# Copying two query tiles out of PSUM ahead of their 1/rms, and a 1/rms formed with tokens on the partitions

## The chip, the cores and the metric

The kernel runs on one core of a Trainium2 chip. The metric is the device time of one execution in microseconds, as the median of several executions. One further execution was taken by the hardware profiler; its rows are the ones quoted below, and their times count from the start of its span.

## What is computed

One step of one decoder layer for two sets of tokens that share the weights: a prompt of 1024 tokens and 64 sample tokens (8 sequences of 8), with 1024 channels in fp32. Cut to what matters here:

```
h = RMSNorm(x)
q, k, v, gmlp_u, gmlp_v, gate_attn, gate_gmlp = split(h @ w_in)
A = sliding-window attention (window 128, grouped queries, a learned sink per head)
B = gelu(gmlp_u) * (W_s LayerNorm(gelu(gmlp_v)) + b)      in chunks of 128 positions
x = x + (sigmoid(gate_attn) * (A @ w_pa) + sigmoid(gate_gmlp) * (B @ w_pb)) @ w_out
x = x + ConvFFN(RMSNorm(x))         up-projection, causal convolution of width 3, gelu gate, down
y = RMSNorm(x)
```

RMSNorm divides each token's row by the root of the mean of its squares: 1/rms is one number per token.

## The kernel before

Activations lie transposed: channels on the 128 partitions, in 8 tiles, and tokens along the free dimension. The 1088 tokens are two groups: group 0 has the 64 sample tokens and 512 of the prompt (576), group 1 the other 512. Each product is made three times, from operands split in a high and a low part (`wh`, `wl` for weights, `hm` for normed inputs), so a tile of 128 output channels takes 24 matmuls (`mm3`, L198 to L206). Weights come through class `Weights` (L71): SP loads a raw tile (`wraw`), ScalarE casts it to `wh` (L39), VectorE subtracts for `wl` (L40). Three raw buffers and four pairs of split buffers go round.

The norm of the inputs is split in two. The gain is put on the inputs at once (`h_of`, L344), and 1/rms, which is the same for all output channels, is put on the products when they leave PSUM. `norm1` (L350) makes it: a matmul with a matrix of ones sums the squares over the channels into every partition (`sc`, L320), ScalarE takes the root (L321), VectorE the reciprocal (L322); for the tiles that have tokens on the partitions, one-column matmuls (`pt`, L355) give the same with four columns (L356, L357).

For each group the order is: 8 query tiles, 2 key tiles (`K0`), values as token-major tiles (L500, tokens on the partitions, `vst`), then attention with the 16 gate tiles as filling between its steps, the gMLP branch, the merge, and the output projection, which leaves x1 (`x1_tile`, L891) and the running sum of its squares in `nacc`. The accumulators of these products come from a pool of two (`acc2`, L245, tiles `mm`). Sums and copies that leave PSUM land in a pool of four staging tiles (`stage`, L242, `stg`).

In group 0, tiles 0 and 1 are copied out of PSUM by ScalarE (L434), `norm1` is called, and then L446 multiplies the copies by 1/rms and 1/8. In group 1 there is no copy. Both tiles run seven eighths of their products, then the last eighth of each (which needs the last of the normed inputs), `norm1` is called, and L446 reads both tiles from PSUM. After query tile 4 of group 1, `rstd_of` (L456) also forms the second norm's 1/rms of group 0, in `nacc0`.

That is needed by the half sums (`half_sums`, L550): four pieces, each with two tiles `hx` loaded from x1 of group 0 (L557), multiplied by gain and 1/rms (L558), combined by GpSimd and VectorE into `ht` (L220 to L223) and stored. They stand among the gate tiles in the text.

The up-projection follows as block products in seven instead of eight (the sums of weight blocks, `ws`, are made by GpSimd, L150; seven products of 12 matmuls in `Chain.product`, L1041, with up to three of eight PSUM banks `st` per chain). The first three pairs of channels (`FEW`) run for group 0 alone, because the inputs of group 1 are still being made: after the third product, `rstd_last` (L967) forms the second 1/rms of group 1 with two 512-column matmuls by ones, a root and a reciprocal of 128x512, and `t1_pieces` (L974) hands out twelve pieces, one behind each later product, which multiply the eight tiles `x1g` by gain and 1/rms (L982), make sums and split them.

The text gives the order only roughly. The framework's scheduler puts each engine's instructions into one fixed order ahead of the run, and each engine works its own queue in that order. An instruction that waits holds up all that is behind it on its engine, on SP's queue too, from which all the large DMAs are issued. The program's order after the build can be read for both kernels.

## Time and profile before

| | |
|---|---|
| median of 3 runs | 1667.56 us (1667.0 to 1672.0) |
| profiled execution, its own time | 1669.62 us |
| its span, first to last instruction | 1667.6 us |
| mean granted TensorE clock | 0.988 |
| instructions | 27566 |
| HBM traffic over the span | 165.40 MB read, 39.00 MB written |

The profile names engines PE (TensorE matmuls), PEld (its weight loads), DVE (VectorE), ACT (ScalarE), POOL (GpSimd) and SP (the queue that issues DMAs). A row of the timeline gives start and length in us, engine, line, operation, output and inputs, shapes and count; in square brackets stands how long the engine had been idle and what ended that. The view of waits gives who waited for whom: total, times, longest. A row of one line's view gives the shortest, median and longest duration in ns. An fp32 matmul runs as two passes, and so shows twice the count of instructions in the rows of L320, L355, L969 and L970.

### The profile page before, as it was taken

How to read it: one execution, taken by the hardware profiler on the slowest of the kernel's cores; microseconds unless marked ns; L12 is line 12 of the kernel's file. 1: busy time of each engine (PE TensorE's matmuls, PEld its weight loads, DVE VectorE, ACT ScalarE, POOL GpSimd, SP SyncE). 2: the span in 40 equal slices, each digit the busy share in tenths (PEclk: the TensorE clock that was granted, in tenths of full speed). 3: DMA queues.
4: the chain of work that ended last, by engine and by line, in shares of the span. 5: the costliest groups of instructions: out<-in, count | busy, mean ns of one | idle time of the engine just before them, and what ended most of it. 6: DMA issues, size and time to landing. Idle time of an engine off the chain costs nothing.

```text
span 1667.6 us, 27566 instructions
## 1 busy us (share of the span) xinstructions
PE 1614.9 (97%) x10912; PEld 1505.8 (90%) x10912; DVE 1043.2 (63%) x1430; ACT 769.0 (46%) x1492; POOL 442.8 (27%) x520
## 2 busy tenths in 40 slices
PE   8999999999989999999998999999999999999997
PEld 8989999999977888898877989999989999999886
DVE  8546863654467677565466777777777778345433
ACT  6435653333343466444344455545555556344231
POOL 1302230100321344210025555555455541000101
PEclk9999999999989999999999899999999999999998
DMA  5332223144646332424472322231232217744421
GB/s 192 117 115 80 86 86 130 50 150 130 205 137 205 104 101 89 140 83 130 154 255 87 113 104 83 89 106 70 77 105 79 78 62 261 253 149 136 156 91 57
DMA packets 80977, 204.22 MB, mean 122 GB/s; under 512 B 9296, under 2 KB 15504, under 8 KB 80848
## 3 DMA queue, kind: packets, MB, share of 16 engines
q1 hardware_dynamic: 80704, 202.45, 36.3%
q8 instruction: 86, 1.41, 0.3%
q14 instruction: 43, 0.35, 0.1%
q10 hardware_dynamic: 144, 0.01, 0.0%
HBM read 165.40 MB, written 39.00 MB: 123 GB/s over the span
## 4 chain that ended last, share of the span: by engine, by line
PE 77%; DVE 9%; POOL 4%; ACT 4%; DMA 3%; issue 2%; SPq 0%; DVEq 0%; POOLq 0%; ACTq 0%
PE mm L205 30%; PE st L1051 21%; PE dn L1164 15%; PE mm L505 6%; DVE wl L40 2%; POOL ws L150 2%; ACT s L696 1%; PE sc L681 1%; PE po L729 1%; DMA wraw<-wt 1%; POOL pl L717 1%; ACT wh L39 1%; PE mm L817 1%; PE pt L706 1%; DMA traw<-t0d 1%
## 5 line engine op out<-in xcount | busy, mean ns | idle before, releaser
L205 PE MATMUL mm<-hm,wh 128*128 128x320 f32 (+2 forms) x1920 | 430.5, 333 | 13.6 <-DVE stg L446 6.3
L1051 PE MATMUL st<-th,wh 128*128 128x288 f32 (+1 forms) x1232 | 360.7, 293 | 13.7 <-ACT k L1036 12.5
L40 DVE TENSOR_TENSOR wl<-wraw,wh 128x512 fp32r<-128x512 f32 (+3 forms) x279 | 264.7, 965 | 163.5 <-ACT wh L39 159.8
L1051 PE MATMUL st<-th,wl 128*128 128x288 f32 (+1 forms) x1232 | 358.7, 291 | 5.8 <-DVE wl L40 5.8
L39 ACT CAST wh<-wraw 128x512 fp32r<-128x512 f32 (+3 forms) x279 | 210.9, 772 | 330.1 <-PE mm L205 126.5
L1051 PE MATMUL st<-tl,wh 128*128 128x288 f32 (+1 forms) x1232 | 359.1, 292 | 0.0
L205 PEld LDWEIGHTS mm<-hm,wh 128*128 128x128 f32 x1920 | 303.1, 190 | 42.8 <-DVE stg L446 6.7
L205 PE MATMUL mm<-hm,wl 128*128 128x320 f32 (+1 forms) x960 | 265.2, 330 | 0.0
L1164 PE MATMUL dn<-gr,wh 128*128 128x288 f32 (+3 forms) x1088 | 253.1, 324 | 2.3 <-ACT z L1072 2.3
L1051 PEld LDWEIGHTS st<-th,wh 128*128 128x128 f32 x1232 | 236.8, 192 | 16.9 <-ACT k L1036 14.4
L1051 PEld LDWEIGHTS st<-th,wl 128*128 128x128 f32 x1232 | 236.6, 192 | 6.5 <-DVE wl L40 6.5
L1051 PEld LDWEIGHTS st<-tl,wh 128*128 128x128 f32 x1232 | 236.6, 192 | 0.3 <-issue 0.2
L1164 PEld LDWEIGHTS dn<-gr,wh 128*128 128x128 f32 x1088 | 183.1, 188 | 16.3 <-ACT z L1072 2.5
L1164 PE MATMUL dn<-gr,wl 128*128 128x288 f32 (+3 forms) x544 | 175.8, 323 | 0.0
L205 PEld LDWEIGHTS mm<-hm,wl 128*128 128x128 f32 x960 | 159.8, 190 | 14.9
L1164 PEld LDWEIGHTS dn<-gr,wl 128*128 128x128 f32 x544 | 102.3, 188 | 7.0
L505 PE MATMUL mm<-w2h,hm 128*128 128x256 f32 x576 | 104.4, 283 | 1.1 <-DVE vst L44 0.8
L40 DVE TENSOR_TENSOR wl<-ws,wh 128x512 fp32r<-128x512 f32 x100 | 87.2, 888 | 15.4 <-ACT wh L39 14.1
L150 POOL TENSOR_TENSOR ws<-wraw 128x512 f32<-128x512 f32 x50 | 83.3, 1667 | 33.5 <-DVE wl L40 18.2
L505 PEld LDWEIGHTS mm<-w2h,hm 128*128 128x128 f32 x576 | 89.7, 191 | 2.0 <-DVE vst L44 1.0
L1080 DVE SCALAR_TENSOR_TENSOR c<-z,cw,c 128x1104 f32<-128x1104 f32 x44 | 72.7, 1653 | 21.1 <-ACT c L1079 21.1
L205 PE MATMUL mm<-qo,wh 128*128 128x320 f32 (+2 forms) x384 | 84.6, 328 | 0.2 <-DVE stg L825 0.2
(220 smaller groups left out, 2366.4 us busy)
## 6 DMA issues: line engine op xcount, KB each, us to landing
wraw<-wt SPq DMA_DIRECT2D x160, 512.0 KB
wraw<-wt SPq DMA_DIRECT2D x90, 256.0 KB
gd<-z SPq DMA_DIRECT2D x22, 544.0 KB
graw<-gd SPq DMA_DIRECT2D x22, 288.0 KB
wraw<-wpb SPq DMA_DIRECT2D x16, 384.0 KB
graw<-gd SPq DMA_DIRECT2D x22, 256.0 KB
gate<-stg SPq DMA_DIRECT2D x16, 288.0 KB
stg<-gate SPq DMA_DIRECT2D x16, 288.0 KB
```

What stands on the lines that cost most here:

```text
L39: S.copy(hi, src)
L40: V.tensor_sub(lo, src, hi.bitcast(F32))
L150: G.tensor_add(t, x, y)
L205: PE.matmul(ps[:, lo:lo + c1 - c0], u[:, k, :], v[:, c0:c1], start=(k == 0 and i == 0), stop=(k == nk - 1 and i == 2))
L505: PE.matmul(ps, u[:, lo:lo + P], v[:, k, :], start=(k == 0 and i == 0), stop=(k == KD - 1 and i == 2))
L681: PE.matmul(ps[:, h, o0:256], q, kst[kv][:, e, k0:cur + P], start=e == 0, stop=e == 1)
L696: S.activation(s[:, h], s[:, h], AF.Exp, bias=nm[:, h:h + 1], accum_out=dn[:, h:h + 1])
L706: PE.transpose(pt[:, h * P:h * P + P], s[:, h, 0:P], ident)
L717: G.affine_select(t.rearrange("p (h q) -> p h q", h=4), src.bitcast(F32).rearrange("p (h q) -> p h q", h=4), [[0, 4], [-sign, P]], ALU.is_ ...
L1051: PE.matmul(ps, u[:, kk, :], v, start=first and kk + i == 0, stop=kk == 3 and i == 2, skip_group_check=True)
L1080: V.scalar_tensor_tensor(c, z[:, 1:1105], cw[:, i, 1:2], c, ALU.mult, ALU.add)
L1164: PE.matmul(ps, u[:, c, :], v[:, lo:hi], start=f + i == 0, stop=f == NFF - 1 and i == 2, skip_group_check=True)
```

## The change

Two edits. In group 1, query tile 0 now runs all its products, `norm1` is called, and tile 1 runs; ScalarE copies each of the two tiles to a staging tile, in both groups, and VectorE multiplies the copies:

```diff
+                if g == 1:
+                    w2, ps2, f2 = [W.get()], [acc2(), acc2()], []
+                    mm3(ps2[0], chunks, w2[0], hs, 0, KD, KD)
+                    norm1(pro)
+                    w2.append(W.get())
+                    mm3(ps2[1], chunks, w2[1], hs, 0, KD, KD)
+                for c in range(2):
+                    f2.append(stage(n))
+                    S.copy(f2[c], ps2[c][:, base:base + n])
                 if g == 0:
-                    for c in range(2):
-                        f2.append(stage(n))
-                        S.copy(f2[c], ps2[c][:, base:base + n])
-                else:
-                    w2, ps2, f2 = [W.get()], [acc2(), acc2()], []
-                    mm3(ps2[0], chunks, w2[0], hs, 0, KD - 1, KD)
-                    w2.append(W.get())
-                    mm3(ps2[1], chunks, w2[1], hs, 0, KD - 1, KD)
-                    for c in range(2):
-                        mm3(ps2[c], chunks, w2[c], hs, KD - 1, KD, KD)
-                        f2.append(stage(n))
-                norm1(pro)
+                    norm1(pro)
                 for c in range(2):
-                    src = f2[c] if g == 0 else ps2[c][:, base:base + n]
-                    V.scalar_tensor_tensor(f2[c], src, 0.125, rs, ALU.mult, ALU.mult)
+                    V.scalar_tensor_tensor(f2[c], f2[c], 0.125, rs, ALU.mult, ALU.mult)
                     q_tile(c, f2[c])
```

In `rstd_last`, the sums of squares are formed as one column per 128 tokens, with tokens on the partitions, so that root and reciprocal have a shape of 128x4. ScalarE then scales the identity matrix by each column, and a matmul with ones spreads the four diagonals over all partitions, into a PSUM bank that the eight multiplications of `t1_pieces` read:

```diff
         def rstd_last():
-            ps = psu.tile([P, 512], F32, name="st")
-            PE.matmul(ps, ones, nacc, start=True, stop=False)
-            PE.matmul(ps, ones, late["sq"], start=False, stop=True)
-            S.activation(nacc, ps, AF.Sqrt, bias=eps, scale=1.0 / D)
-            V.reciprocal(nacc, nacc)
+            ps, rt = psu.tile([P, 512], F32, name="st"), up.tile([P, 4], F32, name="rt", bufs=1)
+            for i in range(4):
+                for x in (nacc, late["sq"]):
+                    PE.matmul(ps[:, i:i + 1], x[:, i * P:i * P + P], ones[:, 0:1], start=x is nacc,
+                              stop=x is not nacc)
+            S.activation(rt, ps[:, 0:4], AF.Sqrt, bias=eps, scale=1.0 / D)
+            V.reciprocal(rt, rt)
+            rs = psu.tile([P, 512], F32, name="st")
+            for i in range(4):
+                S.activation(nacc[:, i * P:i * P + P], ident, AF.Copy, scale=rt[:, i:i + 1])
+                PE.matmul(rs[:, i * P:i * P + P], ones, nacc[:, i * P:i * P + P], start=True, stop=True)
+            return rs
```

The bank is handed to `t1_pieces` as `rs_last`, and `norm` in it multiplies by `rs_last` where it had `nacc`.

More of the change, by code (lines that the diff above doesn't have):

```diff
@@ L967, in rstd_last, with t1_pieces @@
         def rstd_last():
-            ps = psu.tile([P, 512], F32, name="st")
-            PE.matmul(ps, ones, nacc, start=True, stop=False)
-            PE.matmul(ps, ones, late["sq"], start=False, stop=True)
-            S.activation(nacc, ps, AF.Sqrt, bias=eps, scale=1.0 / D)
-            V.reciprocal(nacc, nacc)
-        def t1_pieces():
+            ps, rt = psu.tile([P, 512], F32, name="st"), up.tile([P, 4], F32, name="rt", bufs=1)
[10 more added lines that the diff above has]
+            return rs
+        def t1_pieces(rs_last):
             t4 = [traw().rearrange("p (k j c) -> p k j c", k=2, j=4) for _ in range(2)]
@@ L981, in norm @@
             def norm(k):
-                V.scalar_tensor_tensor(x1g[k], x1g[k], gains[:, 1, k:k + 1], nacc, ALU.mult, ALU.mult)
+                V.scalar_tensor_tensor(x1g[k], x1g[k], gains[:, 1, k:k + 1], rs_last, ALU.mult, ALU.mult)
                 return x1g[k].rearrange("p (h c) -> p h c", h=2)
@@ L1097, in layer @@
                 if f == 0 and j == 2:
-                    rstd_last()
-                    rest = t1_pieces()
+                    rest = t1_pieces(rstd_last())
                 if rest and 7 * f + j > 3:
```

## The prediction

> **What bounds the kernel now.** The page comes first: which engine fills the span.

> ```profile
> PE 1614.9 (97%) x10912; PEld 1505.8 (90%) x10912; DVE 1043.2 (63%) x1430; ACT 769.0 (46%) x1492; POOL 442.8 (27%) x520
> ```

> TensorE is busy for 97% of the 1667.6 us span, so time can be won only where TensorE stands still or runs slowly. The view of waits, for TensorE, says where that is (total, times, longest):

> ```profile
> PE st L1051 <- ACT k L1036: 12.5, 8, 4.0
> PE mm L205 <- DVE stg L446: 6.3, 1, 6.3
> ...
> PE mm L505 <- DVE vst L44: 0.8, 1, 0.8
> ```

> The 6.3 us of the second row is the longest single wait of all. It lies at the start of the second group. Rows of the timeline there (start, length, engine, line):

> ```profile
> 474.86 0.63 PE L205 MATMUL mm<-hm,wh 128*128 128x512 f32 x2
> 485.37 1.99 ACT L39 CAST wh<-wraw 128x1024 fp32r<-128x1024 f32 x2 [6.08 <-PE mm L205]
> 486.11 1.02 PE L320 MATMUL sc<-pacc,c_ones 128*128 128x512 f32 x2
> 486.97 0.95 PE L355 MATMUL pt<-c_ones,pacc 128*128 128x1 f32 x8
> 489.39 3.35 DVE L322 RECIPROCAL nrs<-nrs 128x512 f32<-128x512 f32 x1 [0.58 <-ACT nrs L321]
> 489.51 1.21 PE L320 MATMUL sc<-nacc,c_ones 128*128 128x320 f32 x4 [1.59 <-ACT rst L356]
> 492.70 3.72 DVE L322 RECIPROCAL nacc<-nacc 128x576 f32<-128x576 f32 x1
> 496.34 1.22 DVE L446 SCALAR_TENSOR_TENSOR stg<-mm,nrs 128x512 f32<-128x512 f32 x2
> 497.02 0.80 PE L205 MATMUL mm<-hm,wh 128*128 128x512 f32 x1 [6.30 <-DVE stg L446]
> ```

> Both accumulators of the pool hold query tiles 0 and 1, and only L446 empties them. L446 needs 1/rms, and on VectorE it stands behind two reciprocals (3.35 and 3.72 us). So tile 2 starts at 497.02, after 1.59 and 6.30 us of idle TensorE. The table of windows (busy time of PE, PEld, DVE, ACT, POOL; granted clock; DMA) adds what follows the idle time:

> ```profile
> 486.10:497.00 10.90, 3.03 (x15) 1.92 (x13) 9.97 (x7) 4.13 (x6) 0.00 (x0) 0.76 0.30 97
> 497.00:502.00 5.00, 4.98 (x12) 3.92 (x13) 4.84 (x7) 2.46 (x4) 1.30 (x1) 0.50 0.11 33
> 560.00:700.00 140.00, 138.63 (x703) 114.24 (x702) 99.03 (x163) 80.57 (x215) 49.61 (x80) 1.00 0.30 102
> 894.90:925.70 30.80, 23.13 (x152) 21.96 (x150) 26.58 (x35) 15.05 (x33) 15.66 (x18) 0.88 0.18 64
> ```

> From 497 to 502 the granted clock is 0.50: half of 5.0 us, 2.5 us, is lost a second time. From 560 on TensorE is full (138.63 of 140 us), so what is won before stays won. The last row is the place of the other edit: there VectorE is busy for 26.58 of 30.80 us and TensorE for only 23.13, so VectorE's queue sets the pace.

> **Part one: the first two query tiles.** Tiles 0 and 1 are 48 products from 474.86 to 486.11: 0.234 us each, 5.63 us a tile. The norm's products end 0.95 us after 486.97, at 487.92: 1.81 us. In the order as built, tile 0 now runs whole, then the norm's products, then tile 1. Tile 0 reaches its last eighth at about 479.8, and the operands for that are ready at 477.85:

> ```profile
> 472.61 5.24 DVE L44 SCALAR_TENSOR_TENSOR hm<-x,c_gains,hm 128x512 fp32r<-128x512 f32 x6
> L434 ACT COPY stg<-mm x2: 641/642/642, 20.2 to 21.0; 128x576 f32<-128x576 f32 x2
> ```

> So tile 0 ends at 480.5, the norm's products at 482.3, tile 1 at about 488.0. ScalarE casts one weight tile (1.0 us, released at tile 0's end), then copies tile 0; the first group's copies took 0.64 us (second row), so the accumulator is free by 482.2. Tile 2 therefore starts at 488.0, right behind tile 1, instead of 497.02: **9.0 us**. Tile 1's copy stands behind one cast and is done by 489.9; tile 3 needs that at 493.6. With the idle time goes the half clock: **2.5 us**. The two products of the first group's norm (1.21 us), until now inside the idle time, go behind tile 4: **+1.2 us**. The two copies cost nothing, because ScalarE is busy for 4.13 of the 10.90 us of the first window; without that cover they would cost 1.3 us.

> The 3.35 us reciprocal is not removed: it starts near 484.1 and ends at 487.4, under tile 1. What each query tile asks of VectorE, from the view that groups instructions (count, busy, mean ns):

> ```profile
> L40 DVE TENSOR_TENSOR wl<-wraw,wh 128x1024 fp32r<-128x1024 f32 x10 | 12.5, 1259 | 6.8 <-ACT wh L39 6.8
> L420 DVE TENSOR_TENSOR qo<-stg,qo 64x512 fp32r<-64x512 f32 x16 | 12.1, 756 | 0.5
> L453 DVE SCALAR_TENSOR_TENSOR stg<-mm,nrs 128x512 f32<-128x512 f32 x6 | 4.1, 686 | 0.9 <-PE mm L205 0.8
> ```

> One subtraction of weights, two of L420 and one evacuation are 3.5 us in 5.63 us of products, so the query tiles themselves are not late. What is late next is the half sums of the first group (hx, ht; L553 to L564). The build moves the reciprocal of nacc behind tile 4 and all eight hx behind tile 6; before, the first ran right behind the idle time. VectorE's order there becomes: tile 6, hx, hx, ht, tile 7, ht, hx, K tile 0, hx, ht, ht, K tile 1, hx, vst, vst, hx, ht, ht, vst, hx, vst. Each hx from the third on waits for a reload of its buffer, with the evacuations queued behind it. The chain of waits and the timeline show such reloads, and what one did:

> ```profile
> 503.91 3.21 DMA hx<-x1d
> 533.06 5.66 DMA hx<-x1d
> 538.81 0.82 DVE L558 SCALAR_TENSOR_TENSOR hx<-hx,c_gains,nacc 128x576 f32<-128x576 f32 x1 [3.08 <-DMA hx<-x1d]
> 540.38 0.70 PE L205 MATMUL mm<-hm,wh 128*128 128x512 f32 x2 [1.20 <-DVE stg L453]
> 548.26 3.47 POOL L465 CAST kst<-kst 64x1024 fp32r<-64x1024 f32 x2 [3.45 <-DVE kst L464]
> 553.56 6.02 PE mm L505 x48
> ```

> A reload takes 3.3 or 5.7 us with its issue, and the long one cost TensorE 1.20 us. I step through the new order with both. TensorE ends tile 6 at 517.3, tile 7 at 523.0, K tile 0 at 528.6, K tile 1 at 534.2, and a token-major tile takes 3.0 us (half of the last row). With 3.3 us, the hx before K tile 0 ends at 529.4, the one before K tile 1 at 533.6. GpSimd's half sum is queued behind two kst copies (3.47 us) and ends at 536.4, so K tile 1 is evacuated at 538.0. Token-major tile 1 needs that accumulator at 537.2: a stall of 0.8. The hx ahead of the first vst makes the next, 0.9. Sum 1.7 us. With 5.7 us the same steps give 2.8 and 2.9, sum 5.7 us. The old stalls of this stretch (1.20 and the 0.8 at vst, 2.0 us) go with the old order.

> Part one: −9.0 −2.5 +1.2 −2.0 = −12.3 us, plus 1.7 or 5.7: −10.6 or −6.6 us. Both reloads have been seen; I take the middle, **−8.6 us**.

> [...]

> **Part two: the second 1/rms.** Rows of the timeline, and two of single lines:

> ```profile
> 893.06 1.02 PE L969 MATMUL st<-nacc,c_ones 128*128 128x512 f32 x2
> 894.37 0.70 PE L1051 MATMUL st<-th,wh 128*128 128x288 f32 x1
> 896.63 0.46 DVE L1062 TENSOR_TENSOR z<-ku,st 128x288 f32<-128x288 f32 x1 [1.73 <-PE st L1051]
> 897.00 3.35 DVE L972 RECIPROCAL nacc<-nacc 128x512 f32<-128x512 f32 x1
> 904.25 1.21 DVE L40 TENSOR_TENSOR wl<-ws,wh 128x512 fp32r<-128x512 f32 x1
> 912.53 0.40 PE L1051 MATMUL st<-th,wh 128*128 128x288 f32 x1 [1.10 <-ACT kn L1038]
> 917.16 0.61 PE L1051 MATMUL st<-th,wl 128*128 128x288 f32 x1 [3.97 <-DVE wl L40]
> L982 DVE SCALAR_TENSOR_TENSOR x1g<-x1g,c_gains,nacc x8: 737/744/1229, 900.4 to 922.0; 128x512 f32<-128x512 f32 x8
> ```

> ```profile
> L357 DVE RECIPROCAL rst<-rst x2: 120/126/131, 28.3 to 492.7; 128x5 f32<-128x5 f32 x1, 128x4 f32<-128x4 f32 x1
> L492 ACT COPY kout<-stg x2: 298/298/298, 547.7 to 550.9; 128x128 f32<-128x128 f32 x2
> ```

> Removed: 3.35 us of reciprocal, for one of 0.12 (L357, the same shape). Added: eight one-column products, 16 passes of 0.12 (8 in 0.95 us at L355), 1.9 us in place of the 1.3 from 893.06 to 894.37; with a change of kind of product the next one moves to about 895.3. The built order then sets a chain. VectorE first takes z, which waits for that product's bank (897.4, was 896.6), then the reciprocal (898.0). ScalarE scales four 128x128 tiles (0.3 each by L492: 899.2). TensorE multiplies them by ones, four products of two passes in among others, about 0.3 to 0.4 each (an estimate from the 0.12 a pass and the gaps around L969): 900.7. So 1/rms is ready **0.3 us later** than before (897.00 + 3.35), although 3.2 us of reciprocal are gone. What is won is that VectorE does the subtraction of 904.25 (1.21 us) while it waits. Its queue, which ends the wait at 917.16, moves by −1.2 +0.4 = **−0.8 us**. Bounds: at best the whole −3.2 us; at worst +1.0, since ScalarE's built order puts kn, for which TensorE waited until 912.53, behind two weight casts, so that the rest of that product starts only near 916.7. I stay near the step by step value.

> The norms (L982) now read 1/rms from PSUM. L453 reads PSUM at 0.69 and L982 takes 0.74: nothing.

> [...]

> **Sum.** −8.6 −0.8 = −9.4 us. The profiled execution took 1669.62 us (span 1667.6), which gives 1660.2; the median of the runs is 1667.56, and I give the forecast against that: **1658.2 us**.

> **Rivals.** (a) *No new stall to speak of*, and part two at its best: −10.6 −3.2, 1653.8 us. For it: SP's new order fetches ten weight tiles ahead of the reloads, so these meet less traffic. Against it: the 5.66 us row. Chance 0.14. (b) *A stall halves the clock*: reloads of 5.7 us, and one stall near 3 us is followed by 5 us at 0.50, as at 497: −6.6 +2.5 −0.8 = −4.9, 1662.7 us. Against it: no stall under 3 us in the rows above is followed by a lower clock. [...] (c) *It doesn't do what it says*: ScalarE's first copy slips behind the table load and square root, or VectorE evacuates tile 2 only after tile 4 is due at 499.2, and TensorE still waits some 6 us: −3, 1664.6 us. The built order speaks against it. Chance 0.06. (d) *Slower*: the half sums, ahead of the K and V evacuations, become the bound. From 3.3 to 5.7 us of reload the stalls grow by 4.0, so 1.7 per us; all that is won (12.3 −1.7 +0.8 = 11.4) is eaten at 3.3 + 6.7 = 10.0 us, and from there the kernel is slower. At 13 us: 1.7 × 3.0 = +5.1, and 2.5 for the clock: 1675.2 us. No row shows over 5.7. Chance 0.04.

> **How the numbers follow.** The forecast has what is left, 0.64; with its own bounds one at a time (reloads of 3.3 to 5.7, part two from −3.2 to +1.0) it spans 1655.8 to 1660.2, and with the long reload and +1.0 together 1662.0. The range takes in (a) and (b): 1653 to 1663 us; (c) and (d), 0.10, stay out. What a measurement of this kernel can tell from no change is about 0.3%, 5.0 us. Faster by more than that: the forecast, (a) and half of (b), 0.84. Within it: the rest of (b) and (c), 0.12. Slower: 0.04.

> **What would show it.** In the profile after: tile 2's first product right behind tile 1's last, with a granted clock of 1.00, or part one is wrong; new waits of L205 and L505 behind hx in the K and V tiles, 1.7 to 5.7 us in all; the norms starting no sooner after the L969 products than before; the wait now ending at 917.16 ending at most 1 us earlier against its neighbours. What would make the forecast wrong: a wait of over 3 us left before tile 2, stalls over 6 us in the V tiles, or part two off by more than 3 us.

## The result, and the profile after

The changed kernel took 1660.53 us (median of 5, 1657.29 to 1662.08) against 1667.56 us before, 7.0 us less by these medians. The ratio over all runs is 0.9951 with an interval of 0.9933 to 0.9969, which is 8.2 us less (5.2 to 11.2). The prediction was 1658.2 us with a range of 1653 to 1663. A second series on another chip (e4_changed_again) gave 0.9943 (0.9930 to 0.9956), 9.5 us less. The profiled execution took 1662.08 us, its span 1660.1.

The page's first row, and rows of the view of waits for TensorE (total, times, longest):

```profile
PE 1616.0 (97%) x10932; PEld 1508.4 (91%) x10932; DVE 1040.6 (63%) x1430; ACT 770.4 (46%) x1498; POOL 438.7 (26%) x520
```

```profile
PE st L1056 <- ACT k L1041: 15.3, 6, 4.1
PE st L1056 <- DVE wl L40: 2.3, 4, 1.0
PE st L1056 <- ACT kn L1043: 1.7, 1, 1.7
PE sc L678 <- DVE s L684: 0.6, 1, 0.6
```

TensorE is as busy as before (1616.0 against 1614.9 us) in a span that is 7.5 us shorter. The row of 6.3 us behind L446 is gone. New is the wait of 0.6 us at a step of attention (L684). The wait behind `kn` is 1.7 us where it was 1.10, the waits for `k` come to 15.3 us where they came to 12.5, and the longest wait for a weight's `wl` is 1.0 us where it was 3.97. Lines have moved: L446 is now L443, L505 L502, L1051 L1056, L982 L987.

**The first place.** Timeline of after (start, length, engine, line; in brackets the idle time before and what ended it):

```profile
476.59 0.63 PE L205 MATMUL mm<-hm,wh 128*128 128x512 f32 x2
483.13 0.58 ACT L439 COPY stg<-mm 128x512 f32<-128x512 f32 x1
485.74 3.35 DVE L322 RECIPROCAL nrs<-nrs 128x512 f32<-128x512 f32 x1 [1.26 <-ACT nrs L321]
```

and the table of windows of after (busy time of PE, PEld, DVE, ACT, POOL; granted clock; DMA):

```profile
482.20:490.00 7.80, 7.80 (x37) 6.17 (x36) 5.30 (x4) 4.08 (x6) 0.00 (x0) 1.00 0.27 102
490.00:502.00 12.00, 12.00 (x52) 9.62 (x52) 8.63 (x12) 6.91 (x11) 0.00 (x0) 1.00 0.25 88
```

The reciprocal of 3.35 us runs under query tile 1, and TensorE has no idle time at all from 482 to 502, at a clock of 1.00. Before, the same stretch held 1.59 + 6.30 us of waiting and 5 us at 0.50.

**The second place.** Timeline of after, from the last evacuation ahead of the norms to the wait that stands at its end in both kernels (969.39 before, after 4.00 us of waiting, at 80.91 us from the start of its L895 at 888.48):

```profile
880.33 0.69 DVE L892 TENSOR_TENSOR x1g<-stg,mm 128x512 f32<-128x512 f32 x1 [3.73 <-PE mm L205]
888.90 0.17 DVE L972 RECIPROCAL rt<-rt 128x4 f32<-128x4 f32 x1
889.11 1.28 ACT L975 ACTIVATE nacc<-c_ident,rt 128x128 f32<-128x128 f32 x4
891.03 1.41 DVE L987 SCALAR_TENSOR_TENSOR x1g<-x1g,c_gains,st 128x512 f32<-128x512 f32 x2 [1.28 <-PE st L976]
914.51 0.40 PE L1056 MATMUL st<-th,wh 128*128 128x288 f32 x1 [2.79 <-ACT k L1041]
958.26 0.61 PE L1056 MATMUL st<-th,wh 128*128 128x288 f32 x1 [4.11 <-ACT k L1041]
```

From L892 to that end are now 77.93 us, 2.98 less. The first norm starts 10.70 us behind L892, where it started 11.90 us behind it (888.48 to 900.38): 1.2 us sooner, not later.

### The profile page after: what moved, and what is told of

Its sections match the earlier page's. It is cut to its first block, busy times and chain, and to the rows that moved or that the text cites. A ratio compares the mean times of both kernels' runs of the same rounds, so it can differ in the third digit from the quotient of the medians.

```text
span 1660.1 us, 27618 instructions
## 1 busy us (share of the span) xinstructions
PE 1616.0 (97%) x10932; PEld 1508.4 (91%) x10932; DVE 1040.6 (63%) x1430; ACT 770.4 (46%) x1498; POOL 438.7 (26%) x520
## 4 chain that ended last, share of the span: by engine, by line
PE 79%; DVE 8%; POOL 5%; ACT 4%; issue 3%; DMA 1%; SPq 0%; DVEq 0%; POOLq 0%; ACTq 0%
PE mm L205 32%; PE st L1056 21%; PE dn L1168 16%; PE mm L502 6%; DVE wl L40 2%; POOL ws L150 2%; ACT s L693 1%; PE sc L678 1%; PE po L726 1%; ACT wh L39 1%; DMA wraw<-wt 1%; POOL pl L714 1%; PE mm L814 1%; POOL ph L714 1%; PE pt L703 1%
## 5 line engine op out<-in xcount | busy, mean ns | idle before, releaser
L205 PE MATMUL mm<-hm,wh 128*128 128x320 f32 (+2 forms) x1920 | 429.8, 332 | 5.7 <-ACT hm L43 5.1
L1056 PE MATMUL st<-th,wh 128*128 128x288 f32 (+1 forms) x1232 | 360.8, 293 | 17.2 <-ACT k L1041 15.3
L39 ACT CAST wh<-wraw 128x512 fp32r<-128x512 f32 (+3 forms) x279 | 210.9, 772 | 348.4 <-PE mm L205 128.3
L40 DVE TENSOR_TENSOR wl<-wraw,wh 128x512 fp32r<-128x512 f32 (+3 forms) x279 | 265.5, 968 | 161.4 <-ACT wh L39 157.8
L1056 PE MATMUL st<-th,wl 128*128 128x288 f32 (+1 forms) x1232 | 359.4, 292 | 2.3 <-DVE wl L40 2.3
L1056 PE MATMUL st<-tl,wh 128*128 128x288 f32 (+1 forms) x1232 | 359.2, 292 | 0.0
L205 PEld LDWEIGHTS mm<-hm,wh 128*128 128x128 f32 x1920 | 302.5, 190 | 34.2 <-ACT hm L43 5.1
L205 PE MATMUL mm<-hm,wl 128*128 128x320 f32 (+1 forms) x960 | 265.0, 330 | 0.0
L1056 PEld LDWEIGHTS st<-th,wh 128*128 128x128 f32 x1232 | 237.2, 193 | 19.9 <-ACT k L1041 16.9
L1056 PEld LDWEIGHTS st<-th,wl 128*128 128x128 f32 x1232 | 236.9, 192 | 3.4 <-DVE wl L40 3.4
L1056 PEld LDWEIGHTS st<-tl,wh 128*128 128x128 f32 x1232 | 237.0, 192 | 0.0
L205 PEld LDWEIGHTS mm<-hm,wl 128*128 128x128 f32 x960 | 159.4, 190 | 14.6
L502 PE MATMUL mm<-w2h,hm 128*128 128x256 f32 x576 | 104.4, 283 | 2.1 <-DVE vst L44 1.2
L40 DVE TENSOR_TENSOR wl<-ws,wh 128x512 fp32r<-128x512 f32 x100 | 87.6, 892 | 16.6 <-ACT wh L39 15.3
L502 PEld LDWEIGHTS mm<-w2h,hm 128*128 128x128 f32 x576 | 89.8, 191 | 2.6 <-DVE vst L44 1.4
L150 POOL TENSOR_TENSOR ws<-wraw 128x512 f32<-128x512 f32 x50 | 81.7, 1634 | 37.6 <-DVE wl L40 21.0
L205 PE MATMUL mm<-qo,wh 128*128 128x320 f32 (+2 forms) x384 | 85.1, 330 | 0.2 <-DVE stg L822 0.2
```

Of the source, the lines that this page charges most:

```text
L39: S.copy(hi, src)
L40: V.tensor_sub(lo, src, hi.bitcast(F32))
L150: G.tensor_add(t, x, y)
L205: PE.matmul(ps[:, lo:lo + c1 - c0], u[:, k, :], v[:, c0:c1], start=(k == 0 and i == 0), stop=(k == nk - 1 and i == 2))
L502: PE.matmul(ps, u[:, lo:lo + P], v[:, k, :], start=(k == 0 and i == 0), stop=(k == KD - 1 and i == 2))
L1056: PE.matmul(ps, u[:, kk, :], v, start=first and kk + i == 0, stop=kk == 3 and i == 2, skip_group_check=True)
```

## The experiments

The executions of one kernel lie 3 to 11 us apart, and such differences arise far from the change too. So two times were read off each profiled execution besides the ratio to the kernel before. *Start* is the start of the last x1 evacuation (L895, in other kernels L892): what the first edit has won by then. *Stretch* is the time from there to the end of the wait of 4 us (969.39 before): what the second edit wins at its place.

| run | what | median us | ratio (interval) | start | stretch |
|---|---|---|---|---|---|
| before | | 1667.56 | | 888.48 | 80.91 |
| after | both edits | 1660.53 | 0.9951 (0.9933 to 0.9969) | 880.33 | 77.93 |
| e4_changed_again | both edits | 1661.35 | 0.9943 (0.9930 to 0.9956) | 878.96 | 77.87 |
| e8_before_again | none | 1671.88 | 0.9999 (0.9989 to 1.0009) | 889.08 | 81.29 |
| e1_tiles_alone | edit 1 | 1665.34 | 0.9959 (0.9947 to 0.9971) | 880.38 | 81.32 |
| e6_copies_alone | only the copies | 1661.41 | 0.9940 (0.9925 to 0.9955) | 880.29 | 81.47 |
| e3_order_alone | only the order | 1660.90 | 0.9937 (0.9925 to 0.9949) | 876.91 | 81.37 |
| e2_rms_alone | edit 2 | 1667.30 | 0.9976 (0.9965 to 0.9986) | 887.94 | 78.38 |
| e5_order_and_rms | order, edit 2 | 1657.92 | 0.9914 (0.9898 to 0.9929) | 877.86 | 78.71 |
| e10_order_rms_hx_two | the same again | 1656.54 | 0.9909 (0.9893 to 0.9925) | 877.53 | 78.52 |
| e9_changed_hx_two | both, `hx` twice | 1659.07 | 0.9926 (0.9913 to 0.9939) | 882.36 | 78.10 |
| e7_reciprocal_twice | one reciprocal more | 1673.97 | 1.0012 (1.0002 to 1.0022) | 890.73 | 85.68 |
| e11_rms_norms_from_sbuf | edit 2, norms from SBUF | 1670.99 | 0.9996 (0.9984 to 1.0008) | 893.45 | 78.83 |
| e12_norms_sbuf_again | the same again | 1669.47 | 1.0001 (0.9989 to 1.0013) | 888.33 | 78.70 |

The kernel before had medians of 1670.05 to 1672.14 on these chips, and each ratio is to runs on its own chip. Four groups stand out. The start has a median of 888.8 in the six kernels with the old first place, 880.3 in the five with copies (8.5 us sooner) and 877.5 in the three with the order alone (11.3 sooner). The stretch is on average 81.3 (80.9 to 81.5) with the old 1/rms and 78.3 (77.9 to 78.7) with the new one read from PSUM: 3.0 us.

A part of every start is chance, because it is there before the changed place is reached: the first product of group 1's tile 0, at 474.86 before, came between 474.45 and 479.20 in the 14 traces. Counted from that product, the last x1 evacuation follows after 413.5 us with the old first place (412.4 to 414.3), after 404.0 with the copies (403.6 to 404.1) and after 400.6 with the order alone (400.5 to 402.2). So edit 1 wins 9.5 us at its place, and the order alone 12.9.

### The two edits apart, and the pair again

e1_tiles_alone has the diff's first hunk and leaves `rstd_last` and `t1_pieces` as before:

> The first edit alone (the two query tiles), the second 1/rms as before. Theory A (the prediction's part one): tile 2 starts right behind tile 1, the last x1_tile addition ends some 9 us earlier than in the kernel before, and since nothing behind it is changed all of that stays: 1658 to 1659 us, ratio 0.9945 to 0.995. Rival B: the up-projection behind it gives back a part of whatever arrives early, so this kernel is no faster than the changed one: 1660.5 us or more. Rival C: both edits share the gain, and this one alone brings 4 to 6 us: 1662 to 1664 us.

e2_rms_alone has the other hunks and leaves the query tiles as before:

> The second edit alone (1/rms with tokens on the partitions), the query tiles as before. In the changed kernel's trace the place itself came out 3 us earlier than the rest (last long VectorE wait of TensorE at 914.5 against 925.7, 11.1 us, of which 8.1 were there before it), and about 3 to 4 us were lost again between 1070 and 1190 us. Theory A: the win stays in part: 1665 to 1667 us, ratio 0.9985 to 0.9995. Rival B: what it wins is given back whole in the up-projection: 1667.6 us, ratio 1.000. Rival C: the loss behind it is larger than the win: over 1669 us.

e4_changed_again is the changed kernel once more:

> The changed kernel once more, for a second trace and a second ratio on the same chip as the other three. If the loss of 3 to 4 us between 1070 and 1190 us is a property of the change, it shows again at the same place, and the ratio is 0.995 again; if it is chance of one execution, the lead of some 11 us at 960 us stays or varies, and the ratio may come out at 0.994 to 0.997.

Measured: edit 1 wins 6.9 us (4.8 to 8.9, from the ratio times 1671.67), edit 2 wins 4.0 us (2.3 to 5.9), both together 9.5 us (7.4 to 11.7). Within the intervals the parts add up. Edit 1 is about what the prediction gave it (8.6), though its ratio, 0.9959, falls short of the 0.9945 to 0.995 expected. Edit 2 is by its ratio, 0.9976, worth more than the 0.9985 to 0.9995 expected, and several times the predicted 0.8 us. The loss between 1070 and 1190 us showed again in e4_changed_again, at the same place; the sum further below comes back to it.

### What the copies are for

e3_order_alone keeps edit 1's order of products but reads both tiles from PSUM, as before. Its diff is against the kernel before:

```diff
                         S.copy(f2[c], ps2[c][:, base:base + n])
+                    norm1(pro)
                 else:
                     w2, ps2, f2 = [W.get()], [acc2(), acc2()], []
-                    mm3(ps2[0], chunks, w2[0], hs, 0, KD - 1, KD)
+                    mm3(ps2[0], chunks, w2[0], hs, 0, KD, KD)
+                    norm1(pro)
                     w2.append(W.get())
-                    mm3(ps2[1], chunks, w2[1], hs, 0, KD - 1, KD)
+                    mm3(ps2[1], chunks, w2[1], hs, 0, KD, KD)
                     for c in range(2):
-                        mm3(ps2[c], chunks, w2[c], hs, KD - 1, KD, KD)
                         f2.append(stage(n))
-                norm1(pro)
                 for c in range(2):
                     src = f2[c] if g == 0 else ps2[c][:, base:base + n]
```

> The first edit's new order of products without its copies: tile 0 whole, the norm's products, tile 1, and VectorE multiplies both tiles straight out of PSUM as before; the second 1/rms as before. Theory A: the order is what wins, since the reciprocal then ends under tile 1 (489.0 in the changed kernel's trace, tile 1 ends at 490): tile 2 waits only for the two multiplications, 0.7 to 1.3 us, and the kernel is within 1 us of the first edit alone: 1658 to 1660 us. It could even win a little, because the half sums stay early in VectorE's order. Rival B: the copies are what wins, and without them tile 2 waits again for the reciprocals: 1663 us or more.

e6_copies_alone does the reverse: the kernel before with both copies, its order of products kept and `norm1` behind them:

```diff
                         f2.append(stage(n))
+                        S.copy(f2[c], ps2[c][:, base:base + n])
                 norm1(pro)
                 for c in range(2):
-                    src = f2[c] if g == 0 else ps2[c][:, base:base + n]
-                    V.scalar_tensor_tensor(f2[c], src, 0.125, rs, ALU.mult, ALU.mult)
+                    V.scalar_tensor_tensor(f2[c], f2[c], 0.125, rs, ALU.mult, ALU.mult)
```

> The first edit's copies without its new order: both tiles end with their last eighths, the norm's products follow, ScalarE copies both tiles, and the 1/rms comes only then; the second 1/rms as before. Theory A: the accumulators are free about 1 us after tile 0's end, so tile 2 starts right behind the norm's products (no 6.3 us wait, no half clock), VectorE works off its backlog of some 6 us under tiles 2 to 4 and the half sums move behind them as in the first edit: ratio 0.995 to 0.9975, no better than the first edit alone (0.9959). Rival B: the backlog reaches tile 4's accumulator (the evacuation of tile 2 comes after 499) and TensorE waits 1 us or more there: 0.998 or more.

e5_order_and_rms is e3_order_alone with edit 2:

> The first edit's order without its copies, together with the second edit. Theory A (the gains lie at different places of one chain and add up): order alone gave 0.9937, the second edit alone 0.9976, so 0.991 to 0.992, faster than both kernels. Rival B: the second edit's win is used up by what comes early from the first: 0.9937, as order alone.

Either half of edit 1 does its work: 10.5 us (8.5 to 12.5) for the order alone, 10.0 us (7.5 to 12.5) for the copies alone, where edit 1 has both and wins 6.9. The copies alone and edit 1 do not differ in start or stretch (880.29 and 81.47 us, 880.38 and 81.32), and their intervals overlap. So the copies alone, though beyond the 0.995 to 0.9975 expected, are not shown to be better than edit 1. Timeline of e3_order_alone, VectorE and TensorE:

```profile
484.98 3.35 DVE L322 RECIPROCAL nrs<-nrs 128x512 f32<-128x512 f32 x1 [0.78 <-ACT nrs L321]
488.37 0.69 DVE L446 SCALAR_TENSOR_TENSOR stg<-mm,nrs 128x512 f32<-128x512 f32 x1
489.51 0.69 DVE L446 SCALAR_TENSOR_TENSOR stg<-mm,nrs 128x512 f32<-128x512 f32 x1 [0.45 <-PE mm L205]
494.48 3.75 DVE L322 RECIPROCAL nacc<-nacc 128x576 f32<-128x576 f32 x1
501.34 0.82 DVE L558 SCALAR_TENSOR_TENSOR hx<-hx,c_gains,nacc 128x576 f32<-128x576 f32 x1
542.04 0.39 PE L505 MATMUL mm<-w2h,hm 128*128 128x256 f32 x1 [0.88 <-DVE vst L44]
```

The reciprocal is done under tile 1, so L446 empties tile 0 before tile 1 ends (488.37) and tile 1 right behind it; there is nothing left for a copy to free sooner. And in the order that the framework makes of this text, the reciprocal of `nacc` stands at 494 and the half sums start at 501, so the stalls among the value tiles are 0.88 us. The same wait was 0.77 us in e10_order_rms_hx_two and 2.08 us in e5_order_and_rms, two traces of one kernel. With the copies the half sums start at 520 or later; the waits among the key and value tiles come to 2.30 us in after, and the new wait of attention adds 0.65. That is 2.1 of the 2.8 us by which the starts differ (880.3 against 877.5); the rest isn't accounted for. The order with edit 2 is the best version: 0.9914 in e5_order_and_rms, 14.4 us less than before, and 0.9909 in e10_order_rms_hx_two, ahead of both kernels.

### Why the half sums stall the value tiles

e9_changed_hx_two gives each half-sum input two buffers in the changed kernel, so that a reload need not wait for its buffer:

```diff
-                        xs = [kvp.tile([P, 576], F32, name=f"hx{e}") for e in range(2)]
+                        xs = [kvp.tile([P, 576], F32, name=f"hx{e}", bufs=2) for e in range(2)]
```

> The changed kernel with two buffers for each half-sum input (hx), so that a half sum's load need not wait until the product before it has read the buffer. Theory A (the copies move the half sums to 520-555 us, where each reload waits for its buffer; the waits of 2.76, 2.21 and 1.39 us on the hx loads in VectorE's queue end in TensorE's stalls of 0.85, 1.23, 0.22 and 0.65 us): these stalls shrink from 2.95 us in all to under 1.5, and the ratio to the kernel before goes from 0.994 to 0.993, some 1.5 us. Theory B (it is the place of the half sums in VectorE's queue, their own running time and the order of what stands behind them, that stalls the token-major products, not the loads): stalls of 2.5 to 3.2 us stay, the ratio stays at 0.994 to 0.995.

e10_order_rms_hx_two ran beside it. In spite of its name it has one buffer each: it is e5_order_and_rms unchanged.

> The second group's order without the copies, with the second 1/rms of the change: once more, as the yardstick for the others of this call. Ratio 0.9914 as in the run before (0.990 to 0.993), a new execution's spread included. Here the half sums run at 501 to 540 us and the stalls among the value tiles are 0.9 us, so both theories of the half sums expect this to be 2 to 3 us ahead of the changed kernel with two buffers if the loads are not the cause (B), and about 1 to 1.5 us ahead if they are (A).

First the changed kernel: GpSimd, VectorE and TensorE in the timeline of after.

```profile
533.88 3.00 POOL L462 CAST kst<-kst 64x1024 fp32r<-64x1024 f32 x2 [0.68 <-DVE kst L461]
536.96 0.81 POOL L221 TENSOR_TENSOR ht<-hx,hx 128x288 f32<-128x288 f32 x1
537.80 0.46 DVE L222 SCALAR_TENSOR_TENSOR ht<-ht,hx 128x288 f32<-128x288 f32 x1 [1.82 <-POOL ht L221]
538.67 0.68 DVE L487 TENSOR_TENSOR stg<-mm,nrs 128x512 f32<-128x512 f32 x1
539.40 0.38 PE L502 MATMUL mm<-w2h,hm 128*128 128x256 f32 x1 [0.85 <-DVE stg L487]
543.76 0.38 PE L502 MATMUL mm<-w2h,hm 128*128 128x256 f32 x1 [1.23 <-DVE vst L44]
546.86 0.82 DVE L555 SCALAR_TENSOR_TENSOR hx<-hx,c_gains,nacc 128x576 f32<-128x576 f32 x1 [2.76 <-DMA hx<-x1d]
```

Then e9_changed_hx_two, VectorE and TensorE:

```profile
538.02 0.46 DVE L222 SCALAR_TENSOR_TENSOR ht<-ht,hx 128x288 f32<-128x288 f32 x1 [0.70 <-POOL ht L221]
538.51 1.17 DVE L223 SCALAR_TENSOR_TENSOR ht<-ht,hx 128x288 f32<-128x288 f32 x1
539.61 1.59 DVE L555 SCALAR_TENSOR_TENSOR hx<-hx,c_gains,nacc 128x576 f32<-128x576 f32 x1
541.12 0.68 DVE L487 TENSOR_TENSOR stg<-mm,nrs 128x512 f32<-128x512 f32 x1
541.85 0.39 PE L502 MATMUL mm<-w2h,hm 128*128 128x256 f32 x1 [1.54 <-DVE stg L487]
546.20 0.39 PE L502 MATMUL mm<-w2h,hm 128*128 128x256 f32 x1 [1.22 <-DVE vst L44]
```

With two buffers no half sum waits for its load any more, and yet the stalls among the key and value tiles stay: 1.54, 1.22 and 0.40 us, 3.16 in all, against 0.85, 1.23 and 0.22, 2.30 us. Ahead of L487 stand, in VectorE's fixed order, the pieces of the half sum: L222 waits for GpSimd's part, which in after is itself queued behind the casts of `kst`, and L223 and `hx` take their time. The wait of 2.76 us for a reload at 546.86 is behind the two large stalls and causes neither. So it is theory B: the place of the half sums in VectorE's queue makes these stalls, not the reload. The later wait of 0.65 us, at attention's L678, did go with the second buffer; in its place stands one of 0.41 us for GpSimd (`po`, L726), which the kernel before has too. Counted from tile 0's first product, the last x1 evacuation comes after 404.0 us, as with one buffer (403.6 to 404.1): nothing is won in all. The ratio, 0.9926, lies 1.7 thousandths below that of the changed kernel, and the intervals overlap; it decides nothing.

### What a reciprocal costs at the second place

e7_reciprocal_twice is the kernel before with one more reciprocal of 128x512, whose result nobody reads:

```diff
             S.activation(nacc, ps, AF.Sqrt, bias=eps, scale=1.0 / D)
+            V.reciprocal(late["sq"], nacc)
             V.reciprocal(nacc, nacc)
```

> The kernel before with its second reciprocal of 128x512 done twice (the additional one writes data that nobody reads), to price a microsecond of VectorE at that place. Theory A (VectorE's queue sets the pace there): 3.35 us more in the queue make the kernel 2.5 to 3.4 us slower, ratio 1.0015 to 1.002, and the waits that ended at 917.2 and 925.7 end that much later. Rival B (the place is set by 1/rms's arrival and by other engines, or the stretch behind it absorbs it): ratio 1.000 to 1.0005.

It costs 2.0 us (0.3 to 3.7) by the ratio, with 2.5 to 3.4 expected by theory A. At the place it costs more than its 3.35 us: the stretch is 85.68 us, 4.4 longer than the 81.3 of its like. Timeline of e7_reciprocal_twice, at the wait that lasted 3.97 us before:

```profile
923.77 0.61 PE L1052 MATMUL st<-th,wl 128*128 128x288 f32 x1 [7.08 <-DVE wl L40]
```

The wait has grown from 3.97 to 7.08 us, by 3.1: what is put on VectorE here comes out at TensorE nearly whole.

e8_before_again is the kernel before against itself, for the size of what such a comparison shows from nothing:

> The kernel before, unchanged, as a kernel of its own: the ratio shows what five rounds can tell (1.000 within 0.0015), and its trace gives the waits of the kernel before on the same chip as the other three: 1.6 and 6.3 us before tile 2, and in the up-projection behind 1060 us the same gaps as in the first trace within 1 us each, if those are not chance.

It gave 0.9999, within 0.1% on either side.

### Where the second 1/rms is read from

e11_rms_norms_from_sbuf is edit 2 alone, but ScalarE copies the spread 1/rms to SBUF and the norms read it there:

```diff
-            return rs
+            S.copy(nacc, rs)
+            return nacc
```

> Edit 2 alone (the second 1/rms with tokens on the partitions), but its spread form is copied by ScalarE to SBUF, so that the eight norms read SBUF alone as they do in the kernel before. Theory A (the gain of edit 2, 4.0 us, is nearly all the shorter chain and the freed VectorE, of which 3.35 us of reciprocal went): the copy adds its running time of some 0.6 to 0.8 us to the chain, single norms may again take 1.16 to 1.23 us beside GpSimd, ratio 0.9976 to 0.9985. Theory B (the norms gain because they no longer share SBUF with GpSimd): most of the gain goes, ratio 0.9990 to 1.0000.

> Edit 2 alone with its spread 1/rms copied to SBUF, once more, because the first look says two things: by the ratio (0.9996, interval 0.9984 to 1.0008) nearly all of edit 2's gain is gone, but by the trace TensorE's lead on the kernel before grows by 2.8 us from 850 to 954 us, nearly as in edit 2 alone (3.3 us), and the 5 us that the execution is behind lie before 545 us, where no line differs. Theory A (the copy costs its place on ScalarE and some slower norms, about 0.5 us at the place): ratio 0.997 to 0.999, and the lead from 850 to 954 us again 2.5 to 3.3 us. Theory B (reading 1/rms from PSUM was most of the gain): ratio 0.9990 to 1.0005 again, and a lead there under 1.5 us.

The view of the norms' line, shortest, median and longest in ns, in e2_rms_alone (from PSUM):

```profile
L990 DVE SCALAR_TENSOR_TENSOR x1g<-x1g,c_gains,st x8: 732/738/748, 898.6 to 918.8; 128x512 f32<-128x512 f32 x8
```

and in e12_norms_sbuf_again (from SBUF), with rows of its timeline:

```profile
L991 DVE SCALAR_TENSOR_TENSOR x1g<-x1g,c_gains,nacc x8: 739/747/1396, 899.7 to 919.3; 128x512 f32<-128x512 f32 x8
```

```profile
915.78 1.40 DVE L991 SCALAR_TENSOR_TENSOR x1g<-x1g,c_gains,nacc 128x512 f32<-128x512 f32 x1
916.58 1.25 POOL L1075 TENSOR_TENSOR z<-kn,k 128x288 f32<-128x288 f32 x1
```

From SBUF, norms that run beside GpSimd take up to 1.40 us; from PSUM none takes over 0.75. At the place this and the copy cost 0.5 us: the stretch is 78.7 and 78.8 us, against 78.3. So of the 3.0 us that edit 2 wins there, the operand's place is 0.5 at most, and at this place theory A holds. The ratios say more, 0.9996 and 1.0001, as if the whole of edit 2's gain were gone, which is theory B. Where the missing 2 to 4 us lie, the traces do not show: in the first of the two, 4.3 of the 5 us that it starts late (893.45) are there before group 1 begins, and in the second start and stretch are those of e2_rms_alone within 0.4 us. Behind the stretch the three take 701.1, 700.8 and 701.0 us to the end of their spans. So the traces show no difference at the end, only the ratios do. This stays open.

## Why the prediction was right, and where it was not

**Tile 2 right behind tile 1: right.** The two waits (1.59 and 6.30 us) are gone and the clock stays at 1.00. Tile 2 starts 13.0 us behind tile 0's first product (476.59 to 489.58) where it started 22.2 us behind it: 9.2 us won, with 9.0 predicted. The copies, 0.58 us each, hide under the products.

**Part one, −8.6 us: right in size.** The start moved by 8.5 us, by 9.5 counted from tile 0's first product, and edit 1 alone won 6.9 (4.8 to 8.9). The new stalls in the key and value tiles come to 2.30 us, between the two values that the steps gave (1.7 and 5.7).

**The reload as the cause of these stalls: wrong.** "Each hx from the third on waits for a reload of its buffer, with the evacuations queued behind it" is what sized them. Two buffers per tile took these waits away and left the stalls (3.16 us). What was right is the step ahead of it, that the half sums are late next, and what the steps with the short reload say of the rest: GpSimd's half sum queued behind the `kst` copies, a stall of 0.8 and one of 0.9 us. Measured are 0.85 and 1.23. What stalls is the queue of half-sum pieces itself, with their waits for GpSimd. Rival (d), with its price per microsecond of reload, had the same wrong lever.

**Part two, −0.8 us: the step that failed.** It measured −3.0 at its place, close to the bound of −3.2. Two statements failed. "1/rms is ready 0.3 us later" became 1.2 us sooner. VectorE in the timeline of e2_rms_alone:

```profile
887.94 0.69 DVE L895 TENSOR_TENSOR x1g<-stg,mm 128x512 f32<-128x512 f32 x1 [3.73 <-PE mm L205]
896.14 0.46 DVE L1070 TENSOR_TENSOR z<-ku,st 128x288 f32<-128x288 f32 x1 [1.74 <-PE st L1059]
896.51 0.17 DVE L975 RECIPROCAL rt<-rt 128x4 f32<-128x4 f32 x1
898.64 1.41 DVE L990 SCALAR_TENSOR_TENSOR x1g<-x1g,c_gains,st 128x512 f32<-128x512 f32 x2 [1.27 <-PE st L979]
```

`z` is no later for the one-column products (8.20 us behind L895, 8.15 before), and from the end of the small reciprocal to the first norm are 1.96 us (896.68 to 898.64) in place of 2.7.

The other, "what is won is that VectorE does the subtraction of 904.25 while it waits", counted only what fits into that one wait. Busy times over the stretch show the rest, one window each; the columns are those of the table of windows. Before:

```profile
888.48:969.39 80.91, 69.12 (x473) 66.24 (x471) 65.96 (x83) 43.01 (x87) 48.52 (x45) 0.92 0.29 97
```

After:

```profile
880.33:958.26 77.93, 66.84 (x493) 64.49 (x491) 61.89 (x83) 43.75 (x91) 48.47 (x45) 0.97 0.30 101
```

e7_reciprocal_twice:

```profile
890.73:976.41 85.68, 69.97 (x472) 66.58 (x470) 69.97 (x84) 42.95 (x87) 47.89 (x45) 0.90 0.28 92
```

VectorE's busy time goes from 65.96 to 61.89 or 69.97 us, by −4.1 and +4.0, and the length of the stretch by −3.0 and +4.8. The prediction had said that VectorE's queue sets the pace here; then its whole saving had to be counted, not one operation of it. The copy's runs go the same way: between e2_rms_alone and e12_norms_sbuf_again VectorE's busy time differs by 1.1 us (62.90 and 63.99), the stretch by 0.3. It isn't one for one: in e11_rms_norms_from_sbuf the busy time (64.86) is only 1.1 us under that of before, and the stretch is 2.1 us shorter. The sign follows in each, the size only roughly.

**The norms from PSUM, "nothing": nearly.** It is worth up to 0.5 us. With 1/rms in SBUF, the norm at 915.78 in e12_norms_sbuf_again took 1.40 us beside GpSimd's L150 and L1075; with 1/rms in PSUM, two norms in e2_rms_alone, from 901.19 on, took 1.39 us together beside GpSimd's L996, and none of the eight took over 0.75.

**"No stall under 3 us in the rows above is followed by a lower clock": too weak a ground.** It says nothing of the stalls that those rows leave out, and the trace of before has such a one, inside the row whose mean was 0.88. Windows of before:

```profile
911.63:915.04 3.41, 0.66 (x3) 0.43 (x3) 2.79 (x3) 1.58 (x4) 3.33 (x4) 1.00 0.06 24
915.04:918.45 3.41, 1.28 (x5) 1.29 (x6) 3.41 (x3) 1.65 (x3) 3.14 (x2) 0.50 0.09 16
921.87:925.28 3.41, 1.50 (x9) 1.03 (x8) 2.79 (x6) 1.81 (x4) 1.22 (x2) 1.00 0.19 74
925.28:928.69 3.41, 3.03 (x11) 2.80 (x12) 3.31 (x7) 1.29 (x3) 1.69 (x1) 0.50 0.23 89
```

The clock halves at 915.04, when the wait of 3.97 us (913.19 to 917.16) is 1.9 us old, and again at 925.28, in a wait of 1.80 us (to 925.66) with one of 0.49 us shortly before it. So part of what TensorE does in this stretch is done at half clock, and edit 2, which splits the long wait, saves some of that as well: TensorE's busy time falls from 69.12 to 66.84 us although edit 2 adds 20 matmul passes. How the 3.0 us divide between clock and waits differs from execution to execution: the granted clock of the stretch is 0.97 in after and 0.99 in e4_changed_again, the same kernel, with TensorE busy for 66.84 and 65.61 us. Rival (b), with the 0.12 that the other chances leave, did not come: the longest stall of after among the key and value tiles was 1.23 us, and its clock is 1.00 from 490 to 575.

**The sum.** Counted from tile 0's first product, the stretch ends after 494.5 us before, and after 481.7 and 481.8 us in the two traces of the changed kernel. These are 12.8 us won there, 3.4 more than the 9.4 predicted, yet by the ratios the end won 8.2 and 9.5. From the end of the stretch to the end of the span are 698.2 us before and 701.8 and 702.0 now: 3.7 us are given back. "What is won before stays won" holds for edit 1, whose kernels without edit 2 take 698.3 to 699.0 us there; for what edit 2 wins it does not hold, and the prediction has no term for that. Most of the loss lies between 1060 and 1120 us, in the up-projection. Before and after, the same wait:

```profile
1076.62 0.39 PE L1051 MATMUL st<-th,wh 128*128 128x256 f32 x1 [1.37 <-ACT k L1036]
```

```profile
1067.51 0.39 PE L1056 MATMUL st<-th,wh 128*128 128x256 f32 x1 [2.79 <-ACT k L1041]
```

and the same 60 us around it in both:

```profile
1062.00:1122.00 60.00, 55.91 (x444) 55.07 (x444) 46.16 (x53) 31.26 (x62) 32.97 (x37) 1.00 0.30 103
```

```profile
1052.90:1112.90 60.00, 54.67 (x410) 53.97 (x409) 44.64 (x51) 30.12 (x59) 32.31 (x33) 0.94 0.28 97
```

The wait is 1.4 us longer, and the clock, 1.00 there before, is now 0.94: TensorE gets through 410 matmuls in place of 444. In the kernels with the new 1/rms this wait is 2.0 to 2.8 us, in the others 1.4 to 1.7. The way from the end of the stretch to the end of the span is 698.5 to 702.0 us with the new 1/rms (over 700 in seven of eight) and 696.7 to 699.0 with the old one. In e2_rms_alone's one trace that takes up all that edit 2 had won, though its twelve runs are 4.0 us ahead by the ratio. No run was made on the cause, so how much of edit 2's 3.0 us lasts to the end stays open. Together: parts too small by 3.4 us, and 3.7 us given back that the prediction doesn't have, cancel. That the time came out closer than its terms is luck.

## What to carry to other kernels

A wait on one engine at the end of a chain can be removed by ordering alone, as the 1.59 and 6.30 us were in e3_order_alone: start the norm's chain one tile earlier, so that it runs under that tile, and no copy is needed to free the accumulator; then look at what the build moved for it. Where an engine's queue sets the pace over a long stretch, price an edit by the engine's busy time over the whole stretch, not by the wait at which it first shows, and look behind the stretch for what is given back. And split a window whose mean clock is under 1.00 before reasoning from it: the one of 0.88 held steps at 1.00 and at 0.50.

## What was not expected of the hardware

The granted clock fell to 0.50 less than 2 us into a wait. The rows at 911 to 929 above show 0.50 from 915.04 on, 1.9 us into a wait of 3.97 us, and again from 925.28 on, in a wait of 1.80 us. A wait of 2.79 us was followed by 0.50 in after and by 1.00 in e2_rms_alone, at the same product. Windows of after (the wait ends at 914.51), then of e2_rms_alone (it ends at 922.20):

```profile
911.93:915.34 3.41, 0.83 (x6) 0.83 (x7) 2.79 (x6) 1.76 (x4) 1.66 (x2) 1.00 0.23 89
915.34:918.75 3.41, 3.11 (x13) 2.76 (x12) 2.91 (x6) 2.25 (x5) 1.30 (x3) 0.50 0.25 94
```

```profile
917.05:920.47 3.42, 2.12 (x14) 1.88 (x14) 2.47 (x5) 2.38 (x6) 1.62 (x2) 1.00 0.03 13
920.47:923.88 3.41, 1.68 (x12) 1.61 (x12) 3.11 (x7) 0.92 (x2) 1.67 (x2) 1.00 0.25 94
923.88:927.29 3.41, 2.06 (x15) 1.67 (x13) 2.90 (x6) 3.09 (x7) 0.56 (x3) 1.00 0.23 89
```
